# One planned order for every engine's queue in a hybrid decoder step

## The chip, the cores and the metric

The kernel runs on one core of a Trainium2 chip, as one program, with single-precision inputs and outputs. The metric is the device time of one execution in microseconds; of the kernel before there are three runs, and their median counts. A separate execution was profiled, and all rows below come from it.

## The reference

A step of a two-layer decoder: layer 0 mixes with a Mamba-2 SSD block, layer 1 with an RG-LRU block, and each is followed by a squared-ReLU MLP. A prompt of 1024 tokens with 16 meta tokens in front and eight sampled tokens pass through the same weights, 1048 columns together. The width is 1024, the MLP's 4096.

```python
for i in range(DEPTH):                                   # DEPTH = 2
    h = rms_norm(x, norm_mix_pre[i])
    m = ssd_mixer(h, ...) if i % 2 == 0 else rglru_mixer(h, ...)
    x = x + rms_norm(m, norm_mix_post[i])
    h = rms_norm(x, norm_ffn_pre[i])
    x = x + rms_norm(sq_relu_mlp(h, w1[i], w2[i]), norm_ffn_post[i])

def ssd_mixer(u, ...):
    proj = u @ w_in                                      # z, x, B, C, dt
    xbc = silu(causal_conv(xbc)); dt = softplus(dt + dt_bias); a = -dt * exp(a_log)
    # by chunks of 128 rows, 8 groups of 4 heads:
    scores = (C @ B.T) * exp(segsum(a)); y = scores @ (x * dt)
    h = h * exp(sum(a)) + B.T @ (x * dt * decay);  y += (C @ h_before) * exp(cumsum(a))
    y = (y + x * d_skip) * silu(z); y = group_rms_norm(y)
    return y @ w_out

def sq_relu_mlp(x, w1, w2):
    h = relu(x @ w1); return (h * h) @ w2
```

New states of both mixers (convolution rows, SSD state, LRU state) are outputs too.

## The kernel before, in words

**Data.** Activations lie with features on the partitions and the 1048 columns in three pieces of 350, 350 and 348 (`WC`). Each single-precision operand of a large product is split in two half-precision parts, and a product takes three matmuls (hi·hi, hi·lo, lo·hi); `bundle` issues 24 of them for one 128 x 350 output. In three quarters of the MLP, `unit` makes 2 x 2 blocks from seven products of sums instead of eight, with 175 columns each.

**Weights** come in strips of 256 columns. `wlane` and `wconv` handle a strip in steps: SP loads it into `ws` (two buffers), VectorE or ScalarE takes the row maximum `rm`, GpSimd's `partition_all_reduce` spreads it over the partitions (`wgb`), VectorE makes a power of two of it in `strip_scale` (`qw`, `pw`, `sw`, `winv`), and `split` writes the two halves to `wh` (five buffers), ScalarE the high and VectorE the low one. Strips of kinds H and S also get sums of their blocks (`sums`: `wp` by ScalarE and VectorE, then additions on `ws` by GpSimd).

**SSD layer.** Eight groups, one after another. `ssd_group` goes through nine chunks: `pe_a` puts three transposes and the product of B and C into one PSUM bank `tp`; `ew_a` reads it as `xdt`, `xdd` (VectorE), `Bt` (ScalarE) and `cbm` (VectorE); `pe_b` multiplies into `st` and `yo`; `ew_b` updates the state `hst` (a product on GpSimd, a sum on VectorE) and the output `yf`. Between these the projections of the next group run (`fill`). `group_norm` follows as a lane of its own.

**MLP.** `first_phase`, then blocks of `unit`; each block's activation `z` lies in a ring of four buffers (tag `r`), which it shares with the sums `f` of the inputs (`input_sums`, `t_sums`: additions on GpSimd, then `TT` or `HT` by ScalarE and VectorE). Every matmul output is one of eight PSUM banks. `last_phase` closes each half layer, with `boundary` for the norms.

**What sets the order.** The program is written as Python generators, called lanes, that take turns (`tick`), so the order in which instructions are traced is an interleaving by hand. From it the framework makes each engine's queue when it compiles: it simulates the machine with lengths of its own, and of the instructions that are ready it issues the one traced first. A queue then runs strictly in the order made. The kernel bends this in two places. `Body.tab` and `Body.table` chain ScalarE's table functions to one another, so that tables are loaded as seldom as traced. In `start`, between `nc.hold(True)` and `nc.hold(False)`, the wrappers `Queue` and `Engines` (lines 78 to 115) chain each instruction to the one before it on its engine, so that the start runs as written. The profile names line 89 or 92, the wrapper's two calls, for nearly every instruction; rows are therefore told apart by tile names. Where one PSUM bank is read by two engines, the framework makes the later reading wait for the earlier.

Of the kernel before, what the change touches and what calls it, by code (L numbers as in the profile page):

```python
# [1 line left out]

# [1 line left out]

# [6 lines left out]
F32 = mybir.dt.float32  # L11
F16 = mybir.dt.float16
I32 = mybir.dt.int32
AF = mybir.ActivationFunctionType
OP = mybir.AluOpType
AX = mybir.AxisListType
PSUM = bass.MemoryType.PSUM
DRAM = bass.MemoryType.DRAM
# [3 lines left out]
P = 128  # L22
# [36 lines left out]
class Carve:  # L59


    def __init__(self, tiles):
        self.free = [[t, 0] for t in tiles]
# [11 lines left out]
        raise ValueError("no room")  # L75


class Queue:


    def __init__(self, tc, eng):
        self.tc, self.eng, self.hold, self.prev = tc, eng, False, None

    def __getattr__(self, name):
        f = getattr(self.eng, name)

        def call(*args, **kw):
            if self.prev is None:
                r = f(*args, **kw)  # L89
            else:  # L90
                with self.tc.issue_after(self.prev.ins):
                    r = f(*args, **kw)
            if self.hold:
                self.prev = r
            return r

        return call


class Engines:  # L100
    def __init__(self, tc):
        self.nc = tc.nc
        self.scalar, self.vector, self.gpsimd, self.tensor = self.queues = [
            Queue(tc, e) for e in (tc.nc.scalar, tc.nc.vector, tc.nc.gpsimd, tc.nc.tensor)]

    def __getattr__(self, name):
        return getattr(self.nc, name)

    def hold(self, on):
        for q in self.queues:  # L110
            q.hold = on

    def release(self):
        for q in self.queues:
            q.prev = None


class Body:
    def __init__(self, ctx, tc, a):
        self.ctx, self.tc, self.nc, self.a = ctx, tc, Engines(tc), a  # L120
        self.lanes = []
        self.last_tab = None
        self.mmi = 0
        self.yfs = {}

# [10 lines left out]

    def tab(self, *args, **kw):

        if self.last_tab is None or self.nc.scalar.hold:
            self.last_tab = self.nc.scalar.activation(*args, **kw)  # L140
        else:
            with self.tc.issue_after(self.last_tab.ins):
                self.last_tab = self.nc.scalar.activation(*args, **kw)

    def table(self, name):
        if self.last_tab is None:
            self.last_tab = self.nc.scalar.preload_act_table_set(name)
        else:
            with self.tc.issue_after(self.last_tab.ins):
                self.last_tab = self.nc.scalar.preload_act_table_set(name)  # L150


    def setup(self):
        nc, tc, ctx = self.nc, self.tc, self.ctx
# [7 lines left out]
        c = self.const  # L162
# [4 lines left out]
        for pool, parts, name in ((c, SMALL, "small"), (self.yspool, SSMALL, "ssmall")):  # L167
            off, n = offsets(parts)
            t = pool.tile([P, n], F32, name=name)
            nc.sync.dma_start(t, self.a[name])  # L170
            self.v.update({m: t[:, o:o + w] for m, (o, w) in off.items()})
        self.ident = c.tile([P, P], F32, name="ident")
        make_identity(tc.nc, self.ident)
        self.tri = self.yspool.tile([P, P], F32, name="tri")
        nc.gpsimd.memset(self.tri, 1.0)
        nc.gpsimd.affine_select(self.tri, self.tri, pattern=[[1, P]], compare_op=OP.is_ge, fill=0.0,
# [37 lines left out]
        a = self.a  # L214
        self.xT = [a["x01"][0], a["x01"][1], a["x2"]]
        sp = []
        x = lambda g: [(a["w_ssd_in"][3 * g + s], "a" if g + s else "d") for s in range(2)]
# [404 lines left out]
    def ssd(self):  # L622
        nc, tc = self.nc, self.tc
        a, v = self.a, self.v
        alltags = self.mmtags = ["mm0", "mm1", "mm2", "tp", "mm3", "cb", "yo", "st"]
        U = self.upool.tile([P, 2, KT, NV], F16, tag="u", name="U")
        self.uact = lambda k, c: (U[:, 0, k, cols(c)], U[:, 1, k, cols(c)])
        with tc.tile_pool(name="dts", bufs=1) as dts:
            with tc.tile_pool(name="rows", bufs=1, reuse_waits="tile") as rows, \
                    tc.tile_pool(name="tmp", bufs=1, reuse_waits="tile") as tmp:  # L630
                self.rows, self.tmp = rows, tmp
                self.conv = {}
                self.zt = {}
                px = self.start(U)
                dtt = Carve([rows.tile([P, 2, T], F32, tag="yf", name="dtt", bufs=2)
                             .rearrange("p t c -> p (t c)") for _ in range(2)])
                dtp = self.dt_phase(U, dts, dtt, self.wneed())
                next(dtp)
                next(dtp)
                next(dtp)  # L640
                for _ in px:
                    next(dtp, None)
                pe = self.fill(0)
                for i in range(6):
                    next(pe)
                    if i > 2:
                        next(dtp, None)
                nc.release()
                for _ in dtp:
                    pass  # L650
                self.silu_x(0)
                self.table(EXPSET)
                for g in range(G):
                    self.mmtags = ["mm0", "mm1", "mm2", "mm3"]
                    last = g == G - 1
                    if g:
                        pe = self.fill(g)
                    slots = self.ssd_group(g)
                    nslot = 12
                    span = 15 if g else 10  # L660
                    pos = 0
                    for si in range(nslot):
                        next(slots, None)
                        while pos < span * (si + 1) // nslot:
                            next(pe, None)
                            pos += 1
                    for _ in slots:
                        pass
                    if not last:
                        self.silu_x(g + 1)  # L670
                        for _ in pe:
                            pass
                        self.silu_z(g)
                        self.table(EXPSET)
                        self.lanes.append(self.group_norm(g))
                    else:
                        self.mmtags = alltags
                        self.silu_z(g)
                        self.table(EXPSET)
                        self.lanes.append(self.group_norm(g))  # L680
                        for _ in pe:
                            pass
                        self.drain()
        self.open_bnd()
        with tc.tile_pool(name="hb", bufs=1, reuse_waits="tile") as hb:
            self.half_b(hb)
        self.ysctx.close()
# [59 lines left out]
    def start(self, U):  # L747

        nc, rows, tmp, wl = self.nc, self.rows, self.tmp, self.wl
        px = self.proj_x(0, start=True)  # L750
        next(px)
        x0, room = self.start_x(0)
        sq = [rows.tile([P, E + 3], F32, tag=t, name="sq", bufs=n) for t, n in (("conv", 8), ("pre", 2))]
        sq = [t[:, i * CW:(i + 1) * CW] for t in sq for i in range(3)]
        sq.append(tmp.tile([P, CW], F32, tag="gsq", name="sq", bufs=2))
        uf = tmp.tile([P, 2, 8, 128], F32, tag="h0", name="uf").rearrange("p t b n -> p (t b n)")[:, :4 * CW]
        ufs = [uf.rearrange("p (k c) -> p k c", k=4), room]
        nc.hold(True)
        n0 = self.start_norm(U, 0, x0, sq, ufs)
        next(n0)  # L760
        next(wl)
        n1, n2 = (self.start_norm(U, c, self.start_x(c)[0], sq, ufs) for c in (1, 2))
        for x in (n0, wl, n0, wl, n0, wl, n0, wl, wl, n1, wl, px, wl, px, n1, n2, px, n1, n1, n1, wl, px, wl, wl, wl,
                  px, n2, px, n2, n2, n2, wl, wl, px, wl, px, wl):
            next(x)
        nc.hold(False)
        return px

    def dt_phase(self, U, dts, dtt, w):
# [215 lines left out]
    def ssd_group(self, g):  # L985
# [40 lines left out]
        def ew_a(i, tp):  # L1026
# [8 lines left out]
            tv = tp[:Q, :256].rearrange("p (h d) -> p h d", h=4)  # L1035
            nc.vector.tensor_tensor(xdt[:Q], tv, self.dt[:Q, tt, hs, None].to_broadcast([Q, 4, 64]), op=OP.mult)
            nc.vector.tensor_tensor(xdd[:Q], tv, self.dtd[:Q, tt, hs, None].to_broadcast([Q, 4, 64]), op=OP.mult)
            Bt = tmp.tile([P, 128], F32, tag="Bt", name="Bt", bufs=2)
            nc.scalar.activation(Bt[:Q], tp[:Q, 256:384], AF.Copy)
            cbm = tmp.tile([P, 128], F32, tag="cbm", name="cbm", bufs=2)  # L1040
            nc.vector.tensor_tensor(cbm[:Q, :Q], tp[:Q, 384:384 + Q], tri[:Q, :Q], op=OP.mult)
            nc.vector.tensor_tensor(L[:Q, :, :Q], L[:Q, :, :Q], cbm[:Q, None, :Q].to_broadcast([Q, 4, Q]),
                                    op=OP.mult)
            S[i] = xdt, xdd, L, Bt
# [491 lines left out]


@with_exitstack
def tile_trunk(ctx, tc, a):
    b = Body(ctx, tc, a)  # L1540
    b.setup()
    b.ssd()
    b.ffn(0)
    b.lru()
    b.ffn(1)


def _strips(w, ns):
# [102 lines left out]
```

## Time and profile before

| what | value |
|---|---|
| median of three runs | 2876.42 us |
| lowest, highest | 2870.04, 2882.12 us |
| the profiled execution | 2887.62 us |
| its span, first to last instruction | 2885.9 us |
| granted TensorE clock, mean | 0.96 |
| TensorE busy | 2571.2 us, 89% |
| VectorE busy | 2050.4 us, 71% |
| ScalarE busy | 1403.1 us, 49% |
| GpSimd busy | 743.0 us, 26% |

In the profile PE is TensorE, PEld its weight loads, DVE VectorE, ACT ScalarE, POOL GpSimd, SP the queue that issues most DMAs. A name like `z<-z,mm` is output and inputs. A row of waits reads: engine and tile that waited, `<-` who ended the wait, microseconds in total, times, longest. "issue" means that the engine stood and the profile shows nobody it waited for. The clock column is the share of TensorE's full clock that was granted.

### The profile page before, as it was taken

To read this page: it belongs to the slowest core of one execution; us is meant where nothing else is said; L and a number is where in the kernel's file an instruction comes from. 1 tells how busy PE (TensorE), PEld (TensorE's weight loads), DVE (VectorE), ACT (ScalarE), POOL (GpSimd) and SP (SyncE) were. 2 spreads that over 40 slices of the span, in tenths; PEclk is the share of its full clock that TensorE was granted. 3 is DMA by queue.
4 is the path that set the end of the run, shared out by engine and by line. 5 is a ranking of instruction groups with operands and counts; after the bars stand their busy time and mean duration, and the time that the engine had idled before them with its cause. 6 is when DMAs were issued, how large, how long until landed. Compare 5 with 4: busy or idle time off the path is not lost. (4 is left out here: it accounts for less than half of the span.)

```text
span 2885.9 us, 57203 instructions
## 1 busy us (share of the span) xinstructions
PE 2571.2 (89%) x23193; PEld 2025.2 (70%) x23193; DVE 2050.4 (71%) x4682; ACT 1403.1 (49%) x2436; POOL 743.0 (26%) x1036
## 2 busy tenths in 40 slices
PE   4988998899897999878989999988999879989998
PEld 2655665565565666777988986665666879979976
DVE  4878666766862596567878788787695567777776
ACT  4666565665654355335244253567564335244342
POOL 2233222212222103543232210223012543231201
PEclk9999999999999999989999999999999989999999
DMA  3333233223344330011112122210130011111122
GB/s 125 96 119 127 73 127 119 97 93 119 125 151 164 132 144 30 30 34 42 60 60 89 45 96 96 96 68 33 70 124 30 31 45 45 45 45 45 60 72 93
DMA packets 71496, 237.71 MB, mean 82 GB/s; under 512 B 11120, under 2 KB 37152, under 8 KB 50368
## 3 DMA queue, kind: packets, MB, share of 16 engines
q1 hardware_dynamic: 64848, 199.35, 20.3%
q0 software_dynamic: 6384, 34.71, 3.1%
q8 instruction: 181, 2.97, 0.4%
q14 instruction: 83, 0.68, 0.1%
HBM read 194.67 MB, written 39.36 MB: 81 GB/s over the span
## 5 line engine op out<-in xcount | busy, mean ns | idle before, releaser
L89 PEld LDWEIGHTS <-wh 128*128 128x128 f16 x17040 | 1499.2, 99 | 516.3 <-issue 59.8
L89 PE MATMUL mm<-U,wh 128*128 128x350 f16 (+3 forms) x7056 | 993.2, 297 | 20.1 <-ACT rr L89 10.2
L89 PE MATMUL mm<-H,wh 128*128 128x175 f16 (+5 forms) x5664 | 557.4, 253 | 37.0 <-DVE z L89 33.0
L89 PEld LDWEIGHTS <-wp 128*128 128x128 f16 x3888 | 310.8, 99 | 91.1 <-issue 63.9
L89 POOL TENSOR_TENSOR ws<-ws 128x256 f32<-128x256 f32 (+1 forms) x192 | 205.0, 1068 | 328.7 <-DVE wp L89 214.2
L89 DVE TENSOR_TENSOR z<-z,mm 128x175 f32<-128x175 f32 (+3 forms) x648 | 228.4, 370 | 28.9 <-ACT z L89 22.0
L89 POOL PARTITION_ALL_REDUCE wgb<-rm x100 | 50.3, 503 | 683.2 <-issue 296.6
L89 PE MATMUL mm<-U,wp 128*128 128x175 f16 (+1 forms) x1728 | 154.8, 245 | 56.0 <-DVE z L89 51.9
L89 PE MATMUL mm<-TT,wh 128*128 128x175 f16 (+1 forms) x1728 | 164.7, 246 | 9.8 <-ACT TT L89 8.9
L89 ACT ACTIVATE z<-z,ti 128x700 f32<-128x700 f32 (+1 forms) x72 | 63.0, 875 | 184.7 <-DVE z L89 184.7
L89 DVE SCALAR_TENSOR_TENSOR wh<-ws,sw,wh 128x1024 f16<-128x1024 f32 x94 | 127.0, 1368 | 34.0 <-ACT wh L89 34.0
L89 DVE TENSOR_SCALAR qw<-wgb 128x1 f32<-128x1 f32 x103 | 15.5, 151 | 187.0 <-POOL wgb L89 187.0
L89 ACT ACTIVATE L<-L,cs 128x128 f32<-128x128 f32 (+1 forms) x288 | 92.3, 380 | 109.2 <-DMA L<-csd 90.2
L89 DVE SCALAR_TENSOR_TENSOR conv<-pre,ssmall,conv 128x1072 f32<-128x1072 f32 x78 | 120.3, 1543 | 9.6 <-ACT conv L89 9.2
L89 DVE SCALAR_TENSOR_TENSOR wh<-ws,s,wh 128x256 f16<-128x256 f32 x256 | 114.6, 490 | 11.1 <-ACT wh L89 11.1
L89 PE MATMUL mm<-H,wp 128*128 128x175 f16 (+1 forms) x864 | 91.3, 243 | 27.8 <-DVE z L89 22.5
L89 DVE TENSOR_REDUCE rm<-ws 128x1 f32<-128x2048 f32 x40 | 91.3, 2282 | 28.4 <-DMA ws<-w 24.5
L89 ACT ACTIVATE wh<-ws,sw 128x2048 f16<-128x2048 f32 x47 | 93.7, 1995 | 34.6 <-DVE sw L89 27.8
L89 ACT ACTIVATE wh<-ws,s 128x512 f16<-128x512 f32 x128 | 83.0, 710 | 48.6 <-POOL ws L89 23.4
L89 DVE TENSOR_TENSOR ss<-ss,sqt 128x350 f32<-128x350 f32 (+3 forms) x154 | 75.8, 499 | 41.9 <-ACT sqt L89 41.5
L89 DVE TENSOR_TENSOR H<-z,H 128x175 f16<-128x175 f32 (+5 forms) x120 | 82.5, 705 | 22.5 <-ACT H L89 18.4
L89 POOL TENSOR_TENSOR yf<-yf,ex 128x256 f32<-128x256 f32 x64 | 51.4, 803 | 177.4 <-issue 86.1
(274 smaller groups left out, 4134.6 us busy)
## 6 DMA issues: line engine op xcount, KB each, us to landing
ws<-w SPq DMA_DIRECT2D x64, 1024.0 KB, 4.9
ws<-w_ssd_in SPq DMA_DIRECT2D x24, 1024.0 KB, 5.0
L<-csd SPq DMA_DIRECT2D x64, 256.0 KB, 3.5
ws<-w_lru_in SPq DMA_DIRECT2D x12, 1024.0 KB, 5.1
xd<-xc POOLq DMA_DIRECT2D x6, 1400.0 KB, 5.1
xc<-xd SPq DMA_DIRECT2D x6, 1400.0 KB, 5.9
h<-ssd_h SPq DMA_DIRECT2D x8, 1024.0 KB, 5.3
ex<-esd SPq DMA_DIRECT2D x128, 64.0 KB, 3.9
```

The source lines that it names most:

```text
L89: r = f(*args, **kw)
```

## The change

The wrappers `Queue` and `Engines`, `hold` and `release` go; `Body.nc` is the plain engine handle. `tab` and `table` only note their instructions in a list. After the whole program is traced, and before the framework schedules it, the new class `Order` reads the traced instructions and does four things.

`graph` makes nodes: one for an instruction, one for a whole accumulation chain on TensorE. Each has a length from `length` and a latency to a reader on another engine (TensorE 200, VectorE 140, ScalarE 160, GpSimd and SP 100 ns; a DMA 2000 ns and its bytes at 360 per ns, on one channel). Edges are data dependencies, all accesses to one PSUM bank in traced order, the chain of table functions, and the buffers of each tag, which are given out in traced order as earlier tiles are done with. `run` is a list schedule: at each step the engine that is free first takes the ready node with the smallest priority. `apply` runs it four times, each followed by a run backwards in time from whose result the next priorities come, and keeps the shortest. `queue` chains each engine's instructions, SP and GpSimd with their DMA issues among them, in that order, by dependencies that order the queue and add no semaphore.

In `ew_a` the reading of `cbm` moves ahead of that of `Bt`.

```diff
-class Queue:
-    ...
-class Engines:
-    ...
+class Order:
+    ...
+    def length(i, kind, outs, ins):
+
+        n = max([int(np.prod([x[1] for x in list(a.ap)[1:]] or [1])) for a in outs + ins] or [1])
+        scal = sum(all(x[1] == 1 for x in list(a.ap)[1:]) for a in ins)
+        ...
+        if kind == "InstDMACopy":
+            return 350 if eng == "SP" else 600
+        if eng == "PE":
+            c = int(np.prod([x[1] for x in list(outs[0].ap)[1:]]))
+            if ins[0].dtype == F32:
+                t = 2 * max(110, c / 1.2 + 2)
+                return t / 2 if tuple(i.tile_size)[1] < 128 else t
+            return max(30, c / 2.4 + 2.2)
+        if eng == "DVE":
+            ...
+            return 65 + n / 0.96 + 65 * min(scal, 2) * (n > 1) + 80 * (len(outs) > 1)
+        if eng == "Activation":
+            return 90 + 0.83 * n + 90 * scal + 190 * (len(outs) > 1)
+        if kind == "InstPartitionAllReduce":
+            return 600
+        if kind == "InstTensorTensor":
+            return 200 + 2.19 * n
+        return 110 + 6 * n if kind == "InstTensorCopy" else 110 + n
+    ...
+    def node(self, ins, eng, d):
+        ...
+        self.lat.append((200, 140, 160, 100, 100, 0)[eng])
+    ...
+    def run(self, prio, back=False):
+        ...
+        for _ in range(n):
+            t, e = min((free[e] if run[e] else max(free[e], wait[e][0][0]), e) for e in range(6) if run[e] or wait[e])
+            while wait[e] and wait[e][0][0] <= t:
+                i = heapq.heappop(wait[e])[1]
+                heapq.heappush(run[e], (prio[i], i))
+            i = heapq.heappop(run[e])[1]
+            d = dur[i]
+            if self.func[i] and self.func[i] != table:
+                table = self.func[i]
+                d += 1283
+            start[i] = t
+            free[e] = end = t + d
+            ...
+    def apply(self, rounds=4):
+        self.graph()
+        ...
+        for r in range(rounds):
+            start = self.run(prio)
+            if best is None or self.span < best[0]:
+                best = (self.span, start)
+            end = self.run([-s for s in start], back=True)
+            prio = [-s - d for s, d in zip(end, self.dur)]
+            self.say(r)
+        self.queue(best[1])
+    ...
+    def queue(self, start):
+        last = {}
+        info = lambda: mybir.DependencyInfo(mybir.DependencyClass.NoSync, mybir.DependencyReason.DATA)
+        for i in sorted(range(len(self.ops)), key=lambda i: (start[i], i)):
+            o, e = self.ops[i], self.eng[i]
+            if not o:
+                continue
+            if e in last:
+                self.tc.add_manual_dep(o[0], last[e].name, info(), reason="order")
+            last[e] = o[-1]
 
 class Body:
     def __init__(self, ctx, tc, a):
-        self.ctx, self.tc, self.nc, self.a = ctx, tc, Engines(tc), a
+        self.ctx, self.tc, self.nc, self.a = ctx, tc, tc.nc, a
     ...
     def tab(self, *args, **kw):
 
-        if self.last_tab is None or self.nc.scalar.hold:
-            self.last_tab = self.nc.scalar.activation(*args, **kw)
-        else:
-            with self.tc.issue_after(self.last_tab.ins):
-                self.last_tab = self.nc.scalar.activation(*args, **kw)
+        self.tabs.append(self.nc.scalar.activation(*args, **kw).ins)
     ...
-                nc.release()
     ...
-        nc.hold(True)
     ...
-        nc.hold(False)
     ...
         def ew_a(i, tp):
+            cbm = tmp.tile([P, 128], F32, tag="cbm", name="cbm", bufs=2)
+            nc.vector.tensor_tensor(cbm[:Q, :Q], tp[:Q, 384:384 + Q], tri[:Q, :Q], op=OP.mult)
             Bt = tmp.tile([P, 128], F32, tag="Bt", name="Bt", bufs=2)
             nc.scalar.activation(Bt[:Q], tp[:Q, 256:384], AF.Copy)
-            cbm = tmp.tile([P, 128], F32, tag="cbm", name="cbm", bufs=2)
-            nc.vector.tensor_tensor(cbm[:Q, :Q], tp[:Q, 384:384 + Q], tri[:Q, :Q], op=OP.mult)
     ...
+def tile_trunk(tc, a):
+    Order(tc, trace_trunk(tc, a)).apply()
```

More of the change, by code (lines that the diff above doesn't have):

```diff
@@ L1 @@
+import heapq
 from contextlib import ExitStack
+from functools import lru_cache
 import numpy as np
@@ L75, in tile @@
         raise ValueError("no room")
-class Queue:
[L81 to L89, printed above, removed]
-            else:
[L91 to L97, printed above, removed]
@@ L118 @@
 class Body:
     def __init__(self, ctx, tc, a):
-        self.ctx, self.tc, self.nc, self.a = ctx, tc, Engines(tc), a
+        self.ctx, self.tc, self.nc, self.a = ctx, tc, tc.nc, a
         self.lanes = []
-        self.last_tab = None
+        self.tabs = []
         self.mmi = 0
@@ L137, in tab @@
     def tab(self, *args, **kw):
-        if self.last_tab is None or self.nc.scalar.hold:
-            self.last_tab = self.nc.scalar.activation(*args, **kw)
-        else:
-            with self.tc.issue_after(self.last_tab.ins):
-                self.last_tab = self.nc.scalar.activation(*args, **kw)
-    def table(self, name):
[L146 to L150, printed above, removed]
+        self.tabs.append(self.nc.scalar.activation(*args, **kw).ins)
+    def table(self, name):
+        self.tabs.append(self.nc.scalar.preload_act_table_set(name).ins)
     def setup(self):
@@ L172, in setup @@
         self.ident = c.tile([P, P], F32, name="ident")
-        make_identity(tc.nc, self.ident)
+        make_identity(nc, self.ident)
         self.tri = self.yspool.tile([P, P], F32, name="tri")
@@ L1538, in tile_trunk, with trace_trunk @@
 @with_exitstack
-def tile_trunk(ctx, tc, a):
+def trace_trunk(ctx, tc, a):
     b = Body(ctx, tc, a)
@@ L1545, in tile_trunk @@
     b.ffn(1)
+    return b.tabs
+def tile_trunk(tc, a):
+    Order(tc, trace_trunk(tc, a)).apply()
 def _strips(w, ns):
```

254 lines of the change are left out of this document (242 added, 12 removed).

## The prediction

> **What bounds the kernel now.** I read the page first, then the busy time by stage, then who waited for whom on TensorE, and last the order of events around one long wait.
>
> ```profile
> span 2885.9 us, 57203 instructions
> PE 2571.2 (89%) x23193; PEld 2025.2 (70%) x23193; DVE 2050.4 (71%) x4682; ACT 1403.1 (49%) x2436; POOL 743.0 (26%) x1036
> ```
>
> TensorE is the fullest engine, but it stands for 2885.9 - 2571.2 = 315 us. A change that only reorders queues can win that, and no more than that beside what the clock loses. By stage (start; SSD layer; its output product; first MLP; hand-over; LRU; its output; second MLP; end):
>
> ```profile
> 0.00:75.00 75.00, 33.20 (x177) 19.54 (x178) 38.11 (x79) 32.46 (x55) 20.74 (x35) 0.91 0.33 122
> 150.00:900.00 750.00, 669.18 (x4490) 447.02 (x4491) 519.59 (x1274) 435.88 (x819) 199.48 (x308) 0.95 0.35 116
> 900.00:1125.00 225.00, 212.30 (x1390) 136.93 (x1388) 137.91 (x288) 94.31 (x154) 34.05 (x54) 0.98 0.32 120
> 1125.00:1725.00 600.00, 528.61 (x6428) 508.38 (x6427) 443.13 (x1098) 243.51 (x430) 187.42 (x247) 0.95 0.17 58
> 1725.00:1875.00 150.00, 147.28 (x974) 95.03 (x973) 119.90 (x237) 72.71 (x111) 18.31 (x37) 1.00 0.26 93
> 1875.00:2025.00 150.00, 129.75 (x768) 87.36 (x765) 118.71 (x122) 107.98 (x149) 44.01 (x32) 0.93 0.14 49
> 2175.00:2775.00 600.00, 533.42 (x6409) 509.47 (x6407) 426.21 (x1070) 243.53 (x431) 193.24 (x257) 0.95 0.13 45
> 2775.00:2886.00 111.00, 98.60 (x908) 76.92 (x905) 71.43 (x163) 33.87 (x68) 10.65 (x13) 0.96 0.25 88
> ```
>
> The columns are start:end and length, then busy TensorE, weight loads, VectorE, ScalarE, GpSimd, granted clock, DMA share, GB/s. TensorE stands 80.8 us in the SSD layer, 71.4 and 66.6 in the two MLPs, 41.8 in the start, 20.3 in the LRU layer and 12.4 at the end; the rest is about 22. No engine is full in a long stage: VectorE has 443 of 600 in the first MLP. So what holds TensorE is order and latency, not capacity. The clock adds to it: 0.95 in three long stages, where 5% of 669 + 529 + 533 us of busy time is some 87 us; with the start (9% of 33) and the LRU layer (7% of 130) about 99 us, an estimate that takes busy time to shrink as the clock rises.
>
> ```profile
> PE mm L89 <- DVE z L89: 113.1, 70, 6.2
> PE st L89 <- ACT Bt L89: 29.5, 21, 4.2
> PE yo L89 <- DVE ex L89: 24.4, 13, 3.1
> PE mm L89 <- DVE ss L92: 15.0, 1, 15.0
> PE yo L89 <- DVE L L89: 14.1, 17, 1.6
> PE mm L92 <- POOL ss L92: 11.7, 1, 11.7
> PE mm L89 <- ACT rr L89: 10.2, 4, 4.8
> PE mm L89 <- ACT Y L89: 10.0, 4, 6.3
> ```
>
> The MLP waits are for VectorE's additions `z`, which free PSUM banks; the SSD waits (`st`, `yo`, 68 us) are for the small state products' operands.
>
> What lies behind a long MLP wait decides the case. Here are rows of one, by time (start, length, engine, instruction, in brackets the idle time before it):
>
> ```profile
> 1198.15 0.41 POOL L89 PARTITION_ALL_REDUCE wgb<-rm  x1 [5.84 <-issue]
> 1198.60 0.15 DVE L89 TENSOR_SCALAR qw<-wgb 128x1 f32<-128x1 f32 x1 [3.61 <-POOL wgb L89]
> ...
> 1206.13 0.55 POOL L89 TENSOR_TENSOR f<-f 128x175 f32<-128x175 f32 x1 [7.57 <-issue]
> 1207.91 0.65 ACT L89 ACTIVATE TT<-f 128x525 f16<-128x525 f32 x1 [3.39 <-POOL f L89]
> 1208.46 0.29 ACT L89 ACTIVATE z<-mm 128x175 f32<-128x175 f32 x1
> 1211.14 0.33 DVE L89 TENSOR_TENSOR z<-z,mm 128x175 f32<-128x175 f32 x1
> 1211.53 1.05 PE L89 MATMUL mm<-H,wp 128*128 128x174 f16 x6 [4.62 <-DVE z L89]
> ```
>
> GpSimd stands 5.84 us ahead of an all-reduce and 7.57 us behind it, and the profile names nobody it waited for. Its next addition `f` is so late; ScalarE stands at `TT` for it, with the bank copy `z<-mm` queued behind; VectorE's `z` follows, and TensorE has stood 4.62 us. On the other branch VectorE stood 3.61 us at `qw`. Over the run:
>
> ```profile
> POOL wgb L89 <- issue: 296.6, 48, 9.4
> DVE qw L89 <- POOL wgb L89: 187.0, 75, 11.2
> POOL ws L89 <- issue: 96.8, 14, 10.3
> POOL yf L89 <- issue: 86.1, 12, 7.6
> POOL f L89 <- issue: 56.8, 8, 7.7
> ```
>
> The four "issue" rows are 536 us in 82 times, 6.5 us each: a change between all-reduce and elementwise work on GpSimd costs 6 to 7 us that no busy row shows. The Trainium skill has it (GPSIMD Engine Reference, section Instruction dispatch): the first call of a freshly loaded GpSimd routine pays about 6 us, measured 5.95, without a visible instruction. By its figure the 82 times would be 488 us; the rows' 536 includes the way back, which is longer.
>
> **The change, part by part.**
>
> *The plan.* `Order` replaces the framework's choice, the written-out start order and the chains between table functions by one total order for each queue, the DMA issues of SP and GpSimd among them. No work is added or removed on any engine. Its lengths fit VectorE and TensorE well: for 175 columns it has 65 + 182 = 247 ns, plus 140 ns to the reader, so 387 ns from `z` to the next matmul; the rows have 1211.53 - 1211.14 = 0.39 us. For the all-reduce they do not:
>
> ```profile
> L89 POOL PARTITION_ALL_REDUCE wgb<-rm x100 | 50.3, 503 | 683.2 <-issue 296.6 <-DVE rm L89 200.7 <-ACT rstd L89 53.0
> ```
>
> It has 600 ns, which is the busy time of this row and not the 6 to 7 us on either side.
>
> *SSD layer.* An example of what an order can cure:
>
> ```profile
> 545.74 0.26 ACT L89 ACTIVATE Bt<-tp 128x128 f32<-128x128 f32 x1
> 546.05 0.70 PE L89 MATMUL st<-xdd,Bt 128*128 128x256 f32 x2 [3.69 <-ACT Bt L89]
> ```
>
> TensorE stood 3.69 us at `st` while whole projection chains, which need neither `Bt` nor `L`, lay behind it in the queue. A plan that knows when `Bt` comes puts one of them (24 matmuls, 3.6 us) in front. Of the 68 us I take 45, two thirds; bounds 0 (the operands are late by something the plan misjudges) and -68.
>
> *MLPs.* 113.1 us of waits for `z`. The row above shows their root in GpSimd's hidden 6 to 7 us, which the plan cannot see. I take -25, a fifth; bounds 0 and -113.
>
> *Start.* 15.0 + 11.7 us of waits for sums of squares, one wait each. I take -10; bounds 0 and -27. *LRU layer.* 10.2 + 10.0 us of waits; I take -8; bounds 0 and -20.
>
> *Clock.* With a third of the idle time gone I would take a third of 99, but only a quarter of it goes here: -15; bounds 0 and -60.
>
> *The bank's readers.* `cbm` moves ahead of `Bt`.
>
> ```profile
> DVE cbm L89 <- ACT Bt L89: 28.0, 23, 3.1
> L89 DVE TENSOR_TENSOR cbm<-tp,tri 128x128 f32<-128x128 f32 (+1 forms) x72 | 19.5, 271 | 28.1 <-ACT Bt L89 28.0
> ```
>
> VectorE's three readings now follow one another, and 28.0 us of its waits go. `Bt` comes later by one `cbm`, 0.27 us, on the 21 occasions where `st` waits: +5.7. Since VectorE is not full here, I take -5; bounds -28 and +6. If the projections no longer cover `st`, all 72 would pay 0.27 us, +20.
>
> *What the plan loses.* It puts the reader `qw` 0.14 + 0.6 + 0.1 = 0.84 us behind the maximum `rm`, or wherever VectorE has its next gap. Today's order leaves more between them in the SSD layer (first row) than in the MLPs (second and third):
>
> ```profile
> DVE qw L89 <- POOL wgb L89: 11.5, 7, 2.6
> ...
> DVE qw L89 <- POOL wgb L89: 65.0, 25, 5.8
> ...
> DVE qw L89 <- POOL wgb L89: 75.4, 26, 5.7
> ```
>
> With 5.84 us until the all-reduce starts, VectorE would stand up to 5 us at each `qw`, with `xdt`, `cbm`, `L` or `z` queued behind it and TensorE waiting for those. For three strips in each of eight groups that is up to 24 x 5 = 120, less today's 11.5; for the 51 MLP waits, 2.75 us each today, up to 51 x 2.25 = 115. So 0 to +224 us of VectorE standing. In the MLPs TensorE's 113 us for `z` stand against 140 of `qw`, so at most 0.8 of it, +179, reaches TensorE. I take a quarter of that, +45, because the SSD layer's VectorE has 230 us of slack.
>
> *Sum.* -45 - 25 - 10 - 8 - 15 - 5 + 45 = **-63 us**. The profiled execution took 2887.62 us (1.7 around its span), 11.2 above the median 2876.42. So 2887.6 - 63 = 2824.6 in its terms, and **2813** against the median.
>
> **The rivals.**
>
> *The plan holds.* If GpSimd's changes fall where nobody waits, two thirds of the idle time of the four stages goes, 0.67 x (80.8 + 71.4 + 66.6 + 20.3) = 160, with 10 at the start and a third of the clock's loss, 33: 2876 - 203 = **2673**. For it: lengths that meet the rows within a few per cent, and no full engine. Against it: 82 unseen stands of 6.5 us.
>
> *Slower: readers too close to the all-reduce.* The place is VectorE's `qw`. At full price, +179, without the MLPs' 25, the other gains (83) leave +96: **2972**; at two thirds of the price, +119, it is 2912. It decides once the strips cost TensorE more than 108 us beyond today, 1.4 us for each of about 75 strips. For it: VectorE already stands at 75 of the readers, and the SSD layer's cover is an accident of the old order. Against it: a plan's priorities by the remaining path may leave a weight that is not urgent until VectorE is free. By the skill's 5.95 us per load this rival's price would be the same within 2%.
>
> *Nothing.* The old queues already came from a schedule that took whatever was ready; if the rest is latency through four engines, or the buffers handed out by the framework upset the plan (so that it does not do what it says), the time stays: **2876**.
>
> **How the numbers follow.** Forecast 0.40, its own range 2750 to 2862; the plan holds 0.20; nothing 0.13; slower 0.27. A measurement of this kernel tells about 0.5% (14 us) from no change. So faster 0.60, same 0.13, slower 0.27. The range leaves out the lower half of the plan's case and a third of the slower one: 2690 to 2935.
>
> **What would show it.** Right: SSD idle time of TensorE near 35 us and few `st` waits; no `cbm` wait for `Bt`; MLP stages still near 585 us, with `z` waits behind GpSimd's hidden stands; more than 11.5 us of `qw` waits in the SSD layer. Wrong: MLP stages under 560 us (the hidden stands were not the bound), or `qw` waits well over 400 us in total (the slower rival), or a TensorE that stands as long as before for the same operands (nothing).

## The result and the profile after

| | before | after |
|---|---|---|
| median | 2877.53 us | 2953.88 us |
| lowest, highest | 2870.04, 2882.12 us | 2951.16, 2956.49 us |
| span of the profiled execution | 2885.9 us | 2954.8 us |
| TensorE busy | 2571.2 us | 2585.9 us |
| TensorE standing (span less busy) | 314.7 us | 368.9 us |

The ratio is 1.0268 (95% interval 1.0244 to 1.0292): the planned order is 2.7% **slower**. The forecast, 2813, had the wrong sign, and 2953.9 lies above its range. The rival "readers too close to the all-reduce" (2912 to 2972) had the time, with both of its terms too small (below).

The head of the page after, which answers to the first two rows shown of before:

```profile
span 2954.8 us, 57301 instructions
PE 2585.9 (88%) x23193; PEld 2048.1 (69%) x23193; DVE 2089.2 (71%) x4682; ACT 1408.2 (48%) x2436; POOL 764.0 (26%) x1036
```

The counts of TensorE, VectorE, ScalarE and GpSimd are the same, so this is order alone. Of the 68.9 us that the span grew, 54.2 are standing of TensorE and 14.7 are longer busy time at a granted clock of 0.95 instead of 0.96.

**Where it went.** The stages are cut here at the first matmul of a kind, from the views of the tiles `st`, `yA`, `TT`, `xr` and `Y`. The last column of the table is the experiment "told" from below. One such row after, with its first and last start in microseconds:

```profile
L742 PE MATMUL mm<-yA,wh x576: 308/311/500, 898.3 to 1004.2; 128*128 128x350 f16 x128, 128*128 128x348 f16 x64
```

| stage | before | after | difference | told |
|---|---|---|---|---|
| start, to the first `st` | 128.2 | 135.6 | +7.4 | 121.4 |
| SSD layer, to the first `yA` | 723.9 | 762.7 | +38.8 | 665.3 |
| its output product and first blocks, to the first `TT` | 406.0 | 404.6 | -1.4 | 364.8 |
| first MLP and hand-over, to the first `xr` | 620.1 | 639.7 | +19.6 | 600.1 |
| LRU layer, to the first `Y` | 158.7 | 145.5 | -13.2 | 134.5 |
| its output, second MLP and end | 849.0 | 866.7 | +17.7 | 795.0 |
| sum | 2885.9 | 2954.8 | +68.9 | 2681.1 |

The SSD layer, where I expected most of the gain, lost most.

**Who waited.** Some rows of waits of the whole run after, the longest that bear on the question; each has engine, line and tile that waited, who ended it, and microseconds in total, times, longest:

```profile
POOL wgb L545 <- issue: 358.3, 59, 7.9
DVE qw L529 <- POOL wgb L545: 356.2, 67, 15.5
PE mm L677 <- DVE z L1634: 80.9, 35, 5.0
ACT Bt L1317 <- DVE cbm L1315: 62.0, 41, 4.4
PE st L1327 <- ACT Bt L1317: 57.7, 14, 13.5
DVE hst L1345 <- POOL hst L1344: 48.2, 11, 6.8
PE mm L742 <- ACT z L1249: 42.4, 10, 7.2
POOL h L1372 <- DMA h<-ssd_h: 40.3, 6, 7.8
PE mm L677 <- DVE z L1645: 29.8, 12, 4.2
PE mm L677 <- DVE z L1640: 23.0, 23, 7.6
```

VectorE stands 356.2 us at `qw`, the reader of the all-reduce, against 187.0 before and a second row there, that of the wrapper's other line:

```profile
DVE qw L92 <- POOL wgb L92: 13.2, 4, 8.9
```

So 200 us became 356. TensorE's waits for VectorE's `z` are 133.7 us in these three rows and 155.8 in all rows of that kind, against 113.1; `st` waits 57.7 us for `Bt` against 29.5; and the projections of the SSD layer wait 42.4 us for ScalarE's `z`, which no row of before had. The same `qw` row in the window 150 to 900 us (SSD layer), 1150 to 1785 (first MLP) and 2250 to 2850 (second MLP):

```profile
DVE qw L529 <- POOL wgb L545: 106.4, 9, 15.5
...
DVE qw L529 <- POOL wgb L545: 89.6, 20, 7.7
...
DVE qw L529 <- POOL wgb L545: 86.0, 21, 6.8
```

In the SSD layer it was 11.5 us. The two groups of instructions of the page:

```profile
L529 DVE TENSOR_SCALAR qw<-wgb 128x1 f32<-128x1 f32 x109 | 16.5, 152 | 356.7 <-POOL wgb L545 356.2
L545 POOL PARTITION_ALL_REDUCE wgb<-rm x105 | 49.8, 475 | 728.9 <-issue 358.3
```

These all-reduces are busy 49.8 us. GpSimd stands 358.3 us ahead of them with nobody named.

**One of these waits in order of time**, from the SSD layer after (start, length, engine, line, instruction, in brackets the idle time before it and its releaser):

```profile
516.89 3.60 POOL L1372 TENSOR_TENSOR h<-h,decfm 128x2048 f32<-128x2048 f32 x1 [7.78 <-DMA h<-ssd_h]
...
522.55 0.21 PE L1285 MATMUL tp<-conv 128*16 128x16 f32 x2
...
526.32 0.41 POOL L545 PARTITION_ALL_REDUCE wgb<-rm  x1 [5.83 <-issue]
526.76 0.15 DVE L529 TENSOR_SCALAR qw<-wgb 128x1 f32<-128x1 f32 x1 [15.48 <-POOL wgb L545]
...
527.38 2.00 ACT L558 ACTIVATE wh<-ws,sw 128x2048 f16<-128x2048 f32 x1 [7.27 <-DVE winv L548]
...
529.29 1.86 ACT L1249 ACTIVATE z<-mm,undo 128x348 f32<-128x348 f32 x4
...
529.87 6.29 PE L742 MATMUL mm<-U,wh 128*128 128x350 f16 x24 [7.11 <-ACT z L1249]
531.82 0.41 DVE L1312 TENSOR_TENSOR xdt<-tp,dt 16x256 f32<-16x256 f32 x1
...
536.65 0.20 POOL L1164 COPY cvo<-pre 128x24 f32<-128x24 f32 x1 [9.93 <-issue]
...
544.41 0.60 POOL L1344 TENSOR_TENSOR hst<-hst,ecd 128x256 f32<-128x256 f32 x1 [7.55 <-issue]
...
545.04 0.42 DVE L1345 TENSOR_TENSOR hst<-hst,st 128x256 f32<-128x256 f32 x1 [5.43 <-POOL hst L1344]
```

Read it from the end of the product `h` at 520.49. GpSimd then stands 5.83 us to the all-reduce. VectorE has stood at `qw` since 511.28. Behind it lie `winv`, for which ScalarE stands with `wh` and, queued behind that, the bank copies `z`; TensorE stands 7.11 us for those. Also behind it lies `xdt`: the transposes that it reads ended at 522.76, and it starts at 531.82. Later comes the way back: GpSimd's next elementwise product, `hst`, stands 7.55 us, and VectorE 5.43 us for it. Such a `qw` wait of 13.6 to 15.5 us comes six times between 317 and 844 us, about every 105 us. All six have the same history: GpSimd first stands 5.8 to 7.8 us for the load of `h` (40.3 us over the six), then makes the product `h` (3.6 us), and only then changes to the all-reduce. The part of the load that falls into the wait at `qw` is 3.6 to 5.6 us. So about 6 us of each of these long waits are the stand, and the rest is an all-reduce queued behind `h`.

The chain that ended last, by engine, in the page after:

```profile
DVE 25%; PE 21%; issue 15%; POOL 7%; ACT 4%; DMA 2%; SPq 0%; POOLq 0%; DVEq 0%; ACTq 0%
```

15% of the span is time in which the last chain waited for nothing that the profile names. (Before, the chain could be followed over only a fifth of the span, so the shares are not compared.)

### The profile page after: what moved, and what is told of

It is laid out like the page before. It is cut to its first block, busy times and chain, and to the rows that moved or that the text cites. A ratio compares the mean times of both kernels' runs of the same rounds, so it can differ in the third digit from the quotient of the medians.

```text
span 2954.8 us, 57301 instructions
## 1 busy us (share of the span) xinstructions
PE 2585.9 (88%) x23193; PEld 2048.1 (69%) x23193; DVE 2089.2 (71%) x4682; ACT 1408.2 (48%) x2436; POOL 764.0 (26%) x1036
## 4 chain that ended last, share of the span: by engine, by line
DVE 25%; PE 21%; issue 15%; POOL 7%; ACT 4%; DMA 2%; SPq 0%; POOLq 0%; DVEq 0%; ACTq 0%
PE mm L742 17%; DVE wh L562 4%; DVE wp L641 3%; PE mm L677 2%; POOL ws L648 2%; DVE z L1636 2%; DVE z L1640 1%; POOL f L1594 1%; DVE acc L1565 1%; DMA ws<-w 1%; POOL f L1609 1%; DVE z L1637 1%; DVE r L596 1%; DVE H L1516 1%; DVE z L1643 1%
## 5 line engine op out<-in xcount | busy, mean ns | idle before, releaser
L742 PEld LDWEIGHTS <-wh 128*128 128x128 f16 x8832 | 863.3, 99 | 546.7 <-issue 90.0
L742 PE MATMUL mm<-U,wh 128*128 128x350 f16 (+1 forms) x5760 | 912.1, 319 | 74.2 <-ACT z L1249 42.4
L677 PEld LDWEIGHTS <-wh 128*128 128x128 f16 x8640 | 695.8, 100 | 48.0 <-issue 31.2
L677 PE MATMUL mm<-H,wh 128*128 128x175 f16 (+1 forms) x4320 | 385.4, 242 | 24.6 <-DVE z L1640 18.4
L648 POOL TENSOR_TENSOR ws<-ws 128x256 f32<-128x256 f32 (+1 forms) x192 | 225.0, 1172 | 318.0 <-DVE wp L641 287.0
L529 DVE TENSOR_SCALAR qw<-wgb 128x1 f32<-128x1 f32 x109 | 16.5, 152 | 356.7 <-POOL wgb L545 356.2
L545 POOL PARTITION_ALL_REDUCE wgb<-rm x105 | 49.8, 475 | 728.9 <-issue 358.3
L677 PE MATMUL mm<-U,wh 128*128 128x175 f16 (+1 forms) x1728 | 162.6, 246 | 15.4 <-DVE z L1637 10.6
L742 PE MATMUL mm<-H,wh 128*128 128x350 f16 (+3 forms) x1344 | 172.9, 290 | 2.1 <-DVE z L1634 2.1
L558 ACT ACTIVATE wh<-ws,sw 128x2048 f16<-128x2048 f32 (+1 forms) x53 | 104.3, 1968 | 127.4 <-DVE winv L548 85.8
L562 DVE SCALAR_TENSOR_TENSOR wh<-ws,sw,wh 128x1024 f16<-128x1024 f32 (+1 forms) x106 | 139.7, 1347 | 26.9 <-ACT wh L558 26.9
L1162 DVE SCALAR_TENSOR_TENSOR conv<-pre,ssmall,conv 128x1072 f32<-128x1072 f32 x96 | 133.9, 1396 | 7.0 <-ACT conv L1160 5.1
L581 DVE TENSOR_REDUCE rm<-ws 128x1 f32<-128x2048 f32 x41 | 93.4, 2280 | 14.7 <-DMA ws<-w 10.6
L1327 PE MATMUL st<-xdd,Bt 128*128 128x256 f32 (+1 forms) x144 | 49.9, 430 | 59.0 <-ACT Bt L1317 57.7
```

The costliest lines, as they stand in the source:

```text
L558: nc.scalar.activation(w[:, 0, sl], st[:, sl], AF.Copy, scale=s[:, i:i + 1])
L562: nc.vector.scalar_tensor_tensor(w[:, 1, o:o + h], st[:, o:o + h], s[:, i:i + 1], w[:, 0, o:o + h], op0=OP.mult, op1=OP.subtract)
L581: nc.vector.tensor_reduce(rm, st, axis=AX.X, op=OP.max, apply_absolute_value=True)
L648: tt(o, a, b, op=op)
L677: self.nc.tensor.matmul(ps, l, r, start=n == 0, stop=n == len(ops) - 1)
L742: nc.tensor.matmul(ps, l, r, start=first and i == 0, stop=last and i == n - 1)
```

## The experiments

The theory after reading the result (A in the expectations) was that the plan is blind to GpSimd's stands when it changes between the all-reduce and elementwise work: A1 holds the way in alone to blame, A2 the way back alone. The rivals: operands planned too tightly in general, or, for the copies, work that was left out (B); one unlucky plan among many of the same quality; the priorities by remaining path, which the old order did not have (D); and the order of the bank's readers. All ratios are against the kernel before, run beside each.

**The plan is told of the stands (told), and a control (whole).** `run` gets a state: which kind of work GpSimd did last. A change to the all-reduce adds 5.9 us, a change back 7.1 us. The graph also takes strided slices of the tiles `z`, `r` and `f` as whole ranges, so that its dependencies cover those of the framework; "whole" makes that edit alone.

```diff
+        if not isinstance(r, slice) and t.name.split("_")[0] in ("z", "r", "f"):
+            r = slice(int(r[0]), int(r[-1]) + 1)
     ...
+        kind = {"InstPartitionAllReduce": 1, "InstTensorTensor": 2, "InstTensorScalarAffineSelect": 2}
+        self.lib = [kind.get(type(o[0]).__name__, 0) if o and e == 3 else 0 for o, e in zip(self.ops, self.eng)]
     ...
+            if self.lib[i] and self.lib[i] != lib:
+                lib = self.lib[i]
+                d += 5900 if lib == 1 else 7100
```

> The changed kernel whose plan also knows GpSimd's hidden stands: 5900 ns more for an all-reduce behind an elementwise instruction, 7100 ns more for the way back. It also takes the two-by-two slices of the MLP's z, r and f tiles as whole ranges. If the unseen stands made the change slow (theory A), VectorE's waits at qw fall from 356 us to under 150 and the time to 2780-2870. If the plan is slow for another reason, such as operands planned too tightly in general (theory B), the time stays at 2930-2970 with fewer qw waits but as many waits of TensorE.

> Control for the run above: the changed kernel with the whole ranges alone, the hidden stands still unknown to the plan. Every instruction and length is as in the changed kernel, only the plan comes out another way. Theories A and B both expect 2930-2980 and 300 us or more of qw waits; how far it lies from 2954 tells what one plan differs from another by chance.

Told: 2680.76 us, ratio 0.9313 (0.9289 to 0.9337). Whole: 2953.56 us, 1.0266 (1.0243 to 1.0289). The control is another plan, with the same knowledge as the changed kernel, and takes the same time: the loss is no accident of one plan. Two numbers more in the plan are worth 273 us. The page and the waits of "told":

```profile
PE 2519.8 (94%) x23193; PEld 2002.2 (75%) x23193; DVE 2147.4 (80%) x4682; ACT 1418.2 (53%) x2436; POOL 788.5 (29%) x1036
...
POOL wgb L553 <- issue: 185.4, 29, 9.8
...
DVE qw L537 <- POOL wgb L553: 48.8, 22, 7.4
PE mm L685 <- DVE z L1651: 15.9, 13, 2.1
```

VectorE stands 48.8 us at `qw` instead of 356.2, and TensorE's largest wait for an MLP `z` is 15.9. Waits and time both fell further than theory A had asked (under 150 us, 2780 to 2870). The changes are still there: each shows in the trace as a pair of MODIFY_POOL_CONFIG instructions on GpSimd, and there are 157 such pairs here, 163 after and 165 before. They lie where fewer readers wait. Counted over the 105 strips, VectorE does 7.3 us (median) of other work between a maximum `rm` and its reader `qw`; it was 3.2 before and 1.2 after.

**Without the stands at all (copy_old, copy_plan).** In the kernel before and in the changed one a one-column copy on GpSimd takes the place of a strip's all-reduce. This leaves the spread of the maximum over the partitions out of the computation.

```diff
-        nc.gpsimd.partition_all_reduce(gb, gmax, P, RED.absmax)
+        nc.gpsimd.tensor_copy(gb, gmax)
```

> The kernel before with the all-reduce of each strip replaced by a copy of one column on GpSimd: the spread of the maximum over the partitions is left out, so each partition scales its weights by its own maximum. No hidden stands are left but a handful. Both theories expect it faster than the kernel before; A 2740-2800, because about half of TensorE's 315 us of idle time hangs on them; B 2820-2860.

> The changed kernel with the same replacement, so that the plan's GpSimd lengths are true (the spread over the partitions is left out). Theory A: faster than the old order under the same replacement by 40 us or more, 2640-2740. Theory B: still slower than it, 2800 or more.

On the old order 2654.22 us, 0.9228 (0.9208 to 0.9247); on the plan 2575.30 us, 0.8952 (0.8935 to 0.8970). The trace of each has 5 of the MODIFY_POOL_CONFIG pairs left. So the old order is 222 us shorter without the all-reduces and their stands, the plan that doesn't know them 379 us. Both are faster than theory A expected. The 222 are not the stands alone: the 50 us of GpSimd's own work in the all-reduces went too, and the framework made its order anew around the edit. Without the stands the plan is 79 us better than the old order: its length for this step is then right. "Told", which keeps them, is 105 us above that. The two pages' heads, old order and plan:

```profile
PE 2503.3 (94%) x23193; PEld 1981.2 (75%) x23193; DVE 2031.7 (77%) x4682; ACT 1400.8 (53%) x2436; POOL 735.0 (28%) x1036
```

```profile
PE 2479.8 (96%) x23193; PEld 1979.3 (77%) x23193; DVE 2135.3 (83%) x4682; ACT 1410.0 (55%) x2436; POOL 788.0 (31%) x1036
```

**One half of the knowledge (told_in, told_back).** "Told" with one of the two prices set to nothing.

```diff
-                d += 5900 if lib == 1 else 7100
+                d += 5900 if lib == 1 else 0          # told_in
+                d += 0 if lib == 1 else 7100          # told_back
```

> The kernel told with only half of its knowledge: the 5900 ns ahead of an all-reduce are in the plan, the 7100 ns behind it are not. If the reader of the all-reduce is what the plan put too early (theory A1), nearly all of the gain stays: 2680-2740, with under 100 us of qw waits. If the elementwise work behind the all-reduce is (A2: the sums f and z, the state product hst), most of it goes: 2820-2900.

> The other half: 7100 ns for the way back are in the plan, the 5900 ns ahead of an all-reduce are not. A1 expects most of the loss back, 2830-2930, with 250 us or more of qw waits; A2 expects 2680-2760.

Told_in 2842.55 us, 0.9863 (0.9832 to 0.9894): 111 below the changed kernel. Told_back 2802.84 us, 0.9727 (0.9695 to 0.9759): 151 below, between the times that A1 and A2 expected. The sum, 262, is nearly the 273 of both: the halves add up, and neither A1 nor A2 alone is the cause. The waits of each, told_in first:

```profile
DVE qw L537 <- POOL wgb L553: 139.8, 43, 16.8
...
PE st L1335 <- ACT Bt L1325: 77.5, 16, 9.5
```

```profile
DVE qw L537 <- POOL wgb L553: 253.8, 67, 12.1
...
PE st L1335 <- ACT Bt L1325: 14.1, 6, 9.3
```

Knowledge of the way in cuts the waits at `qw`, but leaves `st` waiting for `Bt`. Knowledge of the way back cuts the wait of `st` to 14.1, with 253.8 us left at `qw`. The way back, which the prediction's slower rival left out, is the larger half.

**The reduction on other engines (pe_old, pe_plan).** Nothing is left out: VectorE multiplies the maximum into the unit matrix, TensorE multiplies that by ones, VectorE takes the maximum of the bank. Once on the old order, once under the plan (with the whole ranges).

```diff
-        nc.gpsimd.partition_all_reduce(gb, gmax, P, RED.absmax)
+        dg = ty.tile([P, P], F32, tag="wdg", name="wdg", bufs=1)
+        nc.vector.tensor_scalar(dg, self.ident, gmax, None, op0=OP.mult)
+        ps = self.mm()
+        nc.tensor.matmul(ps[:, :P], self.ones, dg, start=True, stop=True)
+        nc.vector.tensor_reduce(gb, ps[:, :P], axis=AX.X, op=OP.max)
```

> The kernel before with the strip's all-reduce moved off GpSimd and nothing left out: VectorE scales the identity by the column of maxima (128 columns, about 0.2 us), TensorE multiplies it by ones (two passes of 0.11 us), VectorE takes the maximum of the 128 columns (about 0.25 us). A strip pays about 0.6 us more on VectorE and 0.2 on TensorE, 105 strips together 60 and 23 us, of which little lies on the path. Against 2654 us for the copy: theory A 2650-2710. Theory B, by which the copy gained because it left work out: 2800 or more.

> The same replacement in the changed kernel, with the whole ranges, since without them this plan cannot be carried out; the plan's GpSimd lengths are true. Theory A: 2575-2640, the fastest correct kernel so far, and faster than the old order under the same replacement by 40 us or more. Theory B: not faster than it.

On the old order 2925.22 us, 1.0151 (1.0123 to 1.0180), slower: a miss of A's range. Under the plan 2665.35 us, 0.9257 (0.9233 to 0.9282), the **fastest complete version**, though above A's range too. In pe_old the SSD layer gained: the first `yA` comes at 801.0 us instead of 852.1. The MLPs lost more: the first, from `TT` to `xr`, takes 686.0 us instead of 620.1. The largest waits of TensorE in pe_old:

```profile
PE mm L89 <- ACT wh L89: 89.3, 37, 7.8
PE mm L89 <- DVE wh L89: 79.6, 85, 1.9
PE mm L92 <- DVE wdg L92: 23.9, 4, 11.6
```

The weights `wh` come late there. From the end of `wdg` to the small matmul that reads it 19.9 us pass (median of 109), and TensorE is busy with other chains in 90% of that time; under the plan it is 11.9 us. From a maximum `rm` to its reader `qw` the whole step took 7.5 us in the kernel before. That this delay makes the loss fits, but no run tested it; each reduction also takes one of the eight PSUM banks in turn, which is another candidate. The pair shows in any case that taking the stands out is not enough: 2925 us with the old way of ordering, 2665 with a plan made for what replaced them.

**The bank's readers alone (bank_old).** The kernel before, with `cbm` ahead of `Bt` and nothing else.

```diff
+            cbm = tmp.tile([P, 128], F32, tag="cbm", name="cbm", bufs=2)
+            nc.vector.tensor_tensor(cbm[:Q, :Q], tp[:Q, 384:384 + Q], tri[:Q, :Q], op=OP.mult)
             Bt = tmp.tile([P, 128], F32, tag="Bt", name="Bt", bufs=2)
             nc.scalar.activation(Bt[:Q], tp[:Q, 256:384], AF.Copy)
-            cbm = tmp.tile([P, 128], F32, tag="cbm", name="cbm", bufs=2)
-            nc.vector.tensor_tensor(cbm[:Q, :Q], tp[:Q, 384:384 + Q], tri[:Q, :Q], op=OP.mult)
```

> The kernel before with the other part of the change alone: cbm reads the transposes' bank ahead of Bt. VectorE's 28 us of waits at cbm go, Bt comes 0.27 us later. Expected by the prediction's term: 2871 (5 us faster), with bounds 2848 to 2882. If this part made the change slow instead (theory C), 2900 or more.

2847.94 us, 0.9886 (0.9867 to 0.9905): 31 us faster, at the lower bound expected. So on the old order this part of the change helped, and nothing makes it a cause of the loss; no run has the plan without it. All of it is in the SSD layer (first `yA` at 813.0 instead of 852.1, the gap after that stays). TensorE's waits in that layer (130 to 850 us), before and then bank_old:

```profile
PE st L89 <- ACT Bt L89: 28.6, 20, 4.2
PE yo L89 <- DVE ex L89: 24.4, 13, 3.1
PE yo L89 <- DVE L L89: 12.8, 15, 1.6
```

```profile
PE st L89 <- ACT Bt L89: 20.8, 22, 3.4
PE yo L89 <- DVE ex L89: 14.3, 9, 2.3
...
PE yo L89 <- DVE L L89: 3.1, 5, 1.6
```

The waits of `yo` for `L`, which is made with `cbm`, and for `ex` fall by 19.8 us, more than those of `st`, which fall as well (7.8). The framework made the whole order anew around the edit, so the three rows are not the edit alone.

**Priorities (rounds1, told_trace).** `apply` with one round instead of four takes the traced order as priority; once with the lengths as in the change, once with those of "told".

```diff
-    def apply(self, rounds=4):
+    def apply(self, rounds=1):
```

> The changed kernel with one round instead of four: the lengths are the same, the priority of an instruction is its place in the program as traced, and no run backwards in time sets priorities by the path that is left. Theory A (the unknown stands) expects no faster than 2900, since the plan is as blind. Theory D, that the path priorities throw away an interleaving by hand that was good, expects 2860-2885.

> The kernel told with one round: GpSimd's stands are known, priorities are the traced order. If the knowledge alone makes the gain, 2680-2730; if the path priorities carry a good part of it, 2750-2850.

3117.47 us, 1.0823 (1.0802 to 1.0843), and 2852.62 us, 0.9900 (0.9878 to 0.9921). The second lies just above the upper range expected. So D falls: without the priorities by path the blind plan is 164 us worse still, and the plan that knows the stands 172 us worse. Knowledge is worth 265 us with the traced order as priority and 273 with the path priorities; the two effects are nearly independent. The blind one-round plan has the most standing at `qw` of all the runs:

```profile
DVE qw L529 <- POOL wgb L545: 403.5, 77, 12.9
...
PE st L1327 <- ACT Bt L1317: 93.7, 20, 11.5
```

**Twice the true price (told_double).** "Told" with 11.8 and 14.2 us.

```diff
-                d += 5900 if lib == 1 else 7100
+                d += 11800 if lib == 1 else 14200
```

> The kernel told with both stands priced at twice their length (11800 and 14200 ns). If the gain comes from distance between an all-reduce and its readers, too much of it costs little: 2670-2730. If it comes from true lengths, so that a plan with wrong ones is bad in either direction, 2780 or more.

2964.40 us, 1.0284 (1.0261 to 1.0306): all of the gain is gone. So more distance between the all-reduce and its reader is not better in itself. The waits at `qw` are nearly gone (14.6 us), but others took their place:

```profile
PE mm L685 <- ACT wh L566: 58.1, 17, 9.6
PE st L1335 <- DVE hst L1353: 49.1, 18, 9.3
PE mm L685 <- DVE z L1642: 41.7, 24, 7.8
...
POOL hst L1352 <- DVE hst L1353: 181.3, 25, 16.3
```

Weights and states now come late. As I read it, the plan holds other work back for a GpSimd that is free long before the plan's time; what is shown is that lengths twice too long lose about as much as leaving them out (2964 against 2954 us).

## Why the prediction was wrong, point by point

**The step that failed** is the last term, "What the plan loses", taken as +45 with a bound of +179. The place and the mechanism were right: VectorE at `qw`. Its standing grew from 200 to 356 us, +156 of the 224 bounded. But I passed only a quarter of my bound on to TensorE, with VectorE's 230 us of slack in the SSD layer as the cover. That slack was no cover: the order in a queue is strict, and what stood behind `qw` in the example (`winv`, then `wh`, then the bank copies, and `xdt`) is what TensorE needs next. Against the plan that knows, the loss is 273 us: TensorE stands 207.6 us more and is busy 66.1 us longer. The standing alone is above my bound of 179, and that bound held only the way in. The way back (`hst` in the example) is by the two half experiments the larger part. I had also counted only the 82 stands that a row calls "issue"; the trace of the kernel before has 164 changes.

**The slower rival** had the right time, 2912 to 2972, from two terms that were both too small: gains of 83 us, where "told" shows 195, and a price of up to 179, where the runs show 273. The errors nearly cancel (+96 forecast at full price, +76 measured), so its place and sign were right and its time was in part luck. It got its chance of 0.27 because I held against it that priorities by the remaining path might leave a weight until VectorE is free. The plan left less time: a median of 1.2 us of VectorE's work between `rm` and `qw`, against 3.2 before.

**SSD layer**, -45: +38.8. "The plan misjudges the operands" was the zero end of my bound. I let no harm into this term, and so split one mechanism over two terms with different signs. Told, the layer is 58.6 us shorter than before, busy time included, so a gain of about the size taken existed; the plan blind to the stands did not reach it. Part of the six long `qw` waits there is the late load of `h`, which no term of mine had.

**MLPs**, -25: +19.6 and +17.7. I had written that the plan cannot see the root of the `z` waits and booked a gain all the same. Those waits rose from 113.1 to 155.8 us. "Told", with the root in view, leaves 17.6.

**LRU layer**, -8: -13.2, right in sign and near in size; the waits for `rr` and `Y` that I named fell from 20.2 to 9.4 us. **Start**, -10: +7.4, wrong in sign. The two waits for sums of squares that I named fell only from 26.7 to 22.5 us; what made the start longer, no run looked at.

**Bank's readers**, -5 between -28 and +6: on the old order -31 us. The mechanism was right (no `cbm` wait for `Bt` is left; ScalarE's `Bt` waits for `cbm` in its place, 24.9 us there and 62.0 in the changed kernel); the size was not, since I priced `st` and left out `yo`, which waits for `cbm` through `L`.

**Clock**, -15: it fell to 0.95, and the busy time rose by 14.7 us. The term went with the standing, and took its sign.

**"The plan holds"**, 2673, was refuted for this change. Its time is near that of the plan that knows the stands, 2681.

Of the signs that I named for the forecast, the `cbm` waits went and `qw` waits in the SSD layer passed 11.5 us (106.4); the few `st` waits did not come (57.7 us for `Bt`, against 29.5 before). The sign for the slower rival, "`qw` waits well over 400 us", was set too high: 356 were enough.

## What to carry to other kernels

A schedule that is written out is only as good as its lengths, and a busy row is not a length: look for time before and behind an instruction in which its engine waits for nobody, and give the plan that too, at its true size and in both directions. A model that fits the other engines and is wrong by 6 to 7 us for one rare operation can be worse than a looser order, because it packs the readers close to what it takes for a short step. When a cover is booked for a stall, look at what is queued behind the stalled instruction, not at the share of time in which its engine is free.

## What the runs showed of the hardware that was not expected

GpSimd's change between the partition all-reduce and elementwise work costs both ways: 5.83 us in and 7.55 us back in the example. It is paid at every change. In the changed kernel a pair of MODIFY_POOL_CONFIG instructions stands ahead of the first instruction of the other kind 163 times; from the pair to that instruction pass at least 5.5 us on the way in (median 5.8, 81 times) and at least 6.6 us on the way back (median 7.2, 81 times; the one pair at the start of the program is not a change). The rows named "issue" hold only those for which the profile finds no other releaser. In a kernel where GpSimd is busy for 26% of the span, taking all but a few of them out, with the all-reduces, saved 222 us of 2876. The Trainium skill (GPSIMD Engine Reference, section Instruction dispatch) speaks of the first call to a freshly loaded routine, about 6 us with no visible instruction. The way in agrees in size (5.83), and the way back took 7.55 us. That either is a load of code, no run here shows.

Copies do not pay: no such pair stands ahead of one. In the example the copy `cvo` runs at 536.65, after the all-reduce and 0.12 us after ScalarE wrote the `pre` that it reads; GpSimd pays its 7.55 us only at the product behind it. So the row `[9.93 <-issue]` at that copy is an ordinary wait for data that the profile did not name, and not every "issue" is a stand.

The granted TensorE clock went with the standing. It was 0.925 where TensorE was busy 85% of the span (rounds1), 0.95 at 88% (after), 0.977 at 94% (told) and 0.994 at 96% (copy_plan). Its busy time for the same 23193 matmuls went from 2634.6 to 2479.8 us over these four, while its standing went from 481.3 to 92.5 us: both fell together. Two kernels with 90% had 0.953 (told_in) and 0.967 (bank_old): the share alone does not set it. The Trainium skill (TensorE: Matmul & The Clock Gate, section What's actually happening) has the clock set by how busy TensorE was just before, which agrees in direction; no run here varied it by itself.

Open is the share of late transfers in the new waits. In the example the load of `h` landed 8.6 us after its issue, where the plan's length for it is 4.9; over the run GpSimd stood 40.3 us for it, against 16.7 before. In the control it is 39.8 and in "told" 3.4, where another 22.3 us ahead of `h` are called "issue". That plan moved everything else too, so no run separates this from the rest.
